# A conv's vector taps handed out two at a time, and its normalisation moved behind the compression step

## The chip, the cores and the metric

One core of a Trainium2 chip runs the whole program. The metric is the device time of one execution in microseconds (us), as the median of a few runs. The engines are TensorE (PE; its weight loads are PEld), VectorE (DVE), ScalarE (ACT), GpSimd (POOL), and SyncE (SP), whose queue issues the DMAs. Each engine works through its own queue in order and waits on semaphores for the others.

## The reference

One decoder layer over 1024 tokens of 1024 channels, float32. A normalised input `h` is projected once, and the columns feed three head groups:

```
proj = h @ w_in                                   # 1024 x 2712
p_conv, p_nsa, p_rwkv = split(proj)               # 512, 1304, 896 columns
# conv group: u, gate = split(p_conv)
y = causal_dwconv(u * sigmoid(gate), dw_w, dw_b)  # width 31, 256 channels
y = silu(layer_norm(y, ln_g, ln_b))               # over the 256 channels
# sparse attention (8 query heads, 2 KV heads): compressed, selected and windowed branches
# RWKV-7 (4 heads of 64): delta-rule state, group norm, gate
x = x + concat(y_conv, y_nsa, y_rwkv) @ w_out
x = x + (silu(dwconv3(h2 @ w_gate)) * (h2 @ w_up)) @ w_down
return rms_norm(x)
```

## The kernel before, in words

Channels lie on the 128 partitions, tokens along the free axis in two halves of 512. The kernel runs stage after stage: load and normalise `x`, project, attention tiles (with RWKV work between them), output projection, feed-forward. This change concerns the projections, from about 50 to 360 us.

A projection of 128 columns (`proj_T`, L235) is two PSUM banks, one for each half of the tokens, each of 24 matmuls on L229. Inputs and weights are held as a rounded part and a rest, so each of the eight slices of the inner dimension costs three matmuls. `wload` (L210) fetches the weights in two pieces of 256 KB; `split` (L118) makes the two parts of a piece: ACT copies to `whi` (L120), DVE subtracts to `wlo` (L121). There are two buffers of each, so a piece can be split only once the piece two before it has been used. Banks of projections rotate over two PSUM buffers, so a bank starts once the bank two before it has been copied out (for the keys by ACT on L689 and DVE on L690, for the queries by ACT on L818 and L120 and DVE on L121). I count the banks in order: 16 to 23 are the conv's, 24 to 27 the keys, 28 to 35 the queries, 36 and 37 the first piece of the second RWKV pair, 38 and 39 the first compression, 40 to 45 the other three.

The width-31 convolution covers two groups of 128 channels. Group 0 is 31 instructions on DVE over all 1024 tokens, one for each tap (L270, L272). Group 1 is shared: for each tap and each half ACT scales the input into one of two buffers `ctap` (L278), and POOL adds it to the sum (L279): 60 such pairs, after POOL's first tap (L274). So ACT's third scaling waits for POOL's first addition, and so on, and what stands behind it in ACT's queue waits too: weight copies and bank copies.

The normalisation over 256 channels follows for each half: PE sums both groups (L284), DVE subtracts the mean (L287), ACT squares (L289), PE sums (L294), DVE takes a reciprocal root and spreads it (L301), PE broadcasts (L303), then DVE and ACT finish (L306 to L310) and SP stores the result (`md`, L311).

RWKV work is traced with high priority in between: S00, S01 and so on prepare a pair of heads; each has a chain of 62 small POOL instructions (L532, L534) that inverts a triangular matrix, on data that comes back from DRAM (`sN`); V solves, C runs the state.

The order on each engine is not written by hand. A scheduler with its own cost model places the traced instructions, by the order of the string `steps`, priorities and dependences:

```
lora r0 S00 conv taps V00 S01 keys q C00 V01 r1a cmp0 r1b cmp1 r1c S10 C01 ...
```

Of the kernel before, what the change touches and what calls it, by code (L numbers as in the profile page):

```python
# [7 lines left out]
F32 = mybir.dt.float32  # L8
F32R = mybir.dt.float32r
I32 = mybir.dt.int32  # L10
AF = mybir.ActivationFunctionType
ALU = mybir.AluOpType
AX = mybir.AxisListType
PSUM = bass.MemoryType.PSUM
T = 1024
D = 1024
P = 128


class K:  # L20
    def __init__(self, tc, a, out, ctx, bufs=None):
        self.tc, self.nc, self.a, self.out, self.ctx = tc, tc.nc, a, out, ctx
        self.B = dict(b2=20, wraw=2, whi=2, wlo=2, t4=4, rraw=2, cy=2, hx=12, ev=3, cv=2, lora=2, rb=20, at=2, pr=7, rt=2,
                      QS=2, pp=6, q8=2, pT=5, xn=8, ds=((), (0, 1, 2), (3, 4), (5, 6, 7), (8, 9), (10,), (), ()), h2=14, graw=2, prod=5, ft=4, u=4, wr2=4, wfh=3, wfl=3, S=2, p1=2, om=6, grow=2, pre=2, ap=(), wf=("own", "wf", "om"), hd=("vector",) * 4, tq=((0, 1, 2, 3),), ttag=("tr", "rw"),
                      mm=3, tr=2, av=1, rw=2, mm1=2, tr1=2, pm=2, early="00 01", ga=2, gb=1, gc=1, y=16, r4=15, ta=3, tb=4, mid=2, de=dict(S3="gpsimd", T3="vector", T1="gpsimd", T2="gpsimd", T4="vector", S1="gpsimd", S2="gpsimd", S4="gpsimd"), order=(7, 6, 5, 4, 0, 3, 2, 1), sc=0, pk=1280, st="sync", last=5, sub="gpsimd",  steps="lora r0 S00 conv taps V00 S01 keys q C00 V01 r1a cmp0 r1b cmp1 r1c S10 C01 V10 S11 C10 V11 C11", both=0, cm="gpsimd", rpu=(), wo="vector", tap=(0, 31), vt="cv", vs="vector", va={1: (0, 1), 3: (2, 3), 5: (4, 5), 7: (6, 7)}, vq="sync", vl=1, vw=1, t1=("pm", "tr1"), into={6: (6, 2), 4: (4, 2), 3: (3, 1), 2: (2, 1), 1: (1, 1), 0: (0, 1)})
        self.B.update(bufs or {})
        P_ = lambda n, **k: ctx.enter_context(tc.tile_pool(name=n, **k))
        self.cst = P_("cst", bufs=1)
        self.sm = P_("sm", bufs=4)
        self.big = P_("big", bufs=1)  # L30
        self.mcp = tc.tile_pool(name="mc", bufs=1)
        self.mc = self.mcp.__enter__()
        self.dram = P_("dram", bufs=1, space=bass.MemoryType.DRAM)
        self.uid = 0
        self.st = getattr(tc.nc, self.B["st"])
        self.xp = self.psp = None
# [81 lines left out]
    def split(self, hi, lo, src, eng="vector"):  # L118

        self.nc.scalar.activation(hi, src, AF.Copy)  # L120
        getattr(self.nc, eng).tensor_tensor(lo, src, hi.bitcast(F32), op=ALU.subtract)  # L121

    def consts(self):
        nc = self.nc
# [85 lines left out]
    def wload(self, aps, n):  # L210

        nc = self.nc
        his, los = [], []
        for u in range(2):
            raw = self.wt([P, 4, n], "wraw")
            for i, ap in enumerate(aps):
                m = n // len(aps)
                nc.sync.dma_start(raw[:, :, i * m:i * m + m], ap[u * 512:u * 512 + 512].rearrange("(k p) m -> p k m", p=P))
            hi = self.wt([P, 4, n], "whi", F32R)
            lo = self.wt([P, 4, n], "wlo", F32R)  # L220
            self.split(hi, lo, raw)
            his += [hi[:, k, :] for k in range(4)]
            los += [lo[:, k, :] for k in range(4)]
        return his, los
# [19 lines left out]
    def conv_proj(self, hT):  # L244
        nc, w = self.nc, self.a["w_in"][0]
        self.cy = []
        for j in range(2):
# [10 lines left out]
            self.proj_T(w[:, j * P:(j + 1) * P], hT, cu)  # L258
            self.cy.append(y)

    def conv_rest(self):
        nc = self.nc
        acc = [self.t4(name="cacc")[:, 0:T] for _ in range(2)]
        for j in range(2):
            y, t = self.cy[j], acc[j]
            m = self.B["tap"][j]
            for d in range(31):
                w = self.cw[:, j, d:d + 1]
                if d >= m and d == 0:
                    nc.vector.tensor_scalar(t, y[:, 0:T], w, self.cb[:, j:j + 1], op0=ALU.mult, op1=ALU.add)  # L270
                elif d >= m:
                    nc.vector.scalar_tensor_tensor(t, y[:, d:d + T], w, t, op0=ALU.mult, op1=ALU.add)  # L272
                elif d == 0:
                    nc.gpsimd.tensor_scalar(t, y[:, 0:T], w, self.cb[:, j:j + 1], op0=ALU.mult, op1=ALU.add)  # L274
                else:
                    for o in (0, 512):
                        z = self.xt([P, 512], "cv", name="ctap")
                        nc.scalar.activation(z, y[:, o + d:o + d + 512], AF.Copy, scale=w)  # L278
                        nc.gpsimd.tensor_tensor(t[:, o:o + 512], t[:, o:o + 512], z, op=ALU.add)  # L279
        for half in range(2):  # L280
            sl = slice(half * 512, half * 512 + 512)
            pm = self.bank("tr1")
            for j in range(2):
                nc.tensor.matmul(pm, self.ones, acc[j][:, sl], start=j == 0, stop=j == 1)  # L284
            sq = []
            for j in range(2):
                nc.vector.scalar_tensor_tensor(acc[j][:, sl], pm, -1.0 / 256, acc[j][:, sl], op0=ALU.mult, op1=ALU.add)  # L287
                s = self.xt([P, 512], "cv", name="csq")
                nc.scalar.activation(s, acc[j][:, sl], AF.Square)  # L289
                sq.append(s)  # L290
            pv = self.bank("tr1")
            for i in range(4):
                for j in range(2):
                    nc.tensor.matmul(pv[:, i:i + 1], sq[j][:, i * P:(i + 1) * P], self.ones[:, 0:1], start=j == 0, stop=j == 1)  # L294
            v = self.small([P, 4], "cv")
            nc.vector.tensor_scalar(v, pv[:, 0:4], 1.0 / 256, 1e-5, op0=ALU.mult, op1=ALU.add)
            r = self.small([P, 4], "cr")
            self.rsqrt(r, v, [P, 4])
            dg = self.xt([P, 512], "cv", name="cdg")
            for i in range(4):  # L300
                nc.vector.tensor_scalar(dg[:, i * P:(i + 1) * P], self.idn, r[:, i:i + 1], None, op0=ALU.mult)  # L301
            pr = self.bank("tr1")
            nc.tensor.matmul(pr, self.ones, dg, start=True, stop=True)  # L303
# [521 lines left out]
    def attn_tile(self, i):  # L825
# [46 lines left out]
        for br, lo_k, M, vo in ((2, max(0, k1 - 640), self.mwin, 128), (1, 0, self.msel, 0)):  # L872
# [8 lines left out]
            for r in range(4):  # L881
# [7 lines left out]
                for c, (ka, kb) in enumerate(pcs):  # L889
# [6 lines left out]
                    for g in range(2):  # L896
                        pe.matmul(pts[g][:, 0:n], QS[:, r, g, :], KH[g][hf][:, ks], start=True, stop=False)  # L897
                        pe.matmul(pts[g][:, 0:n], QS[:, r, g, :], KL[g][hf][:, ks], start=False, stop=True)  # L898
                    o = ka % 512 - o
# [371 lines left out]

    def build(self):
        order = self.B["order"]
        nc, a = self.nc, self.a
        self.phase("1")
        self.consts()
# [5 lines left out]
        hT = self.T_tiles("hT", (self.x, "hx", self.B["hx"]))  # L1282
# [32 lines left out]
        def chain(j, h):  # L1315
            with self.tc.high_priority(offset=100000):
                self.rwkv_chain(us[j, h])
        steps = dict(lora=lambda: self.rwkv_lora(hT), keys=lambda: self.attn_keys(hT), q=lambda: self.attn_q(hT),
                     cmp=lambda: self.attn_cmp(hT), conv=lambda: self.conv_proj(hT), taps=self.conv_rest, r0=lambda: self.rwkv_proj(0, hT),
                     r1=lambda: self.rwkv_proj(1, hT), cmp0=lambda: self.attn_cmp(hT, (0,)), cmp1=lambda: self.attn_cmp(hT, (1,)),  # L1320
                     r1a=lambda: self.rwkv_proj(1, hT, (0,)), r1b=lambda: self.rwkv_proj(1, hT, (1,)), r1c=lambda: self.rwkv_proj(1, hT, (2,)))
        for st in self.B["steps"].split():
# [15 lines left out]
        grow = [self._t(self.x3, [P, 512], F32, "grow", None) for _ in range(2)]  # L1338
# [67 lines left out]
```

## Time and profile before

| | |
|---|---|
| median of 3 runs | 1483.7 us (1480.32 to 1494.8) |
| profiled execution | 1479.4 us |
| its span in the trace | 1477.5 us |
| PE busy | 1388.7 us (94%) |
| DVE, ACT, POOL busy | 1002.7, 686.9, 499.2 us |
| share of the last-ending chain: PE, DVE, POOL | 79%, 8%, 4% |

PE is busy nearly everywhere, so the span shortens only where PE waits or runs at the lower clock. Of the 40 slices of the page, the three from 148 to 258 us show a granted clock of 8 tenths, and the first of them PE at 5 tenths of busy time. They lie in the stage that the change edits.

### The profile page before, as it was taken

The page shows a single profiled execution, that of the slowest core. Times are in us where ns is not written, and L with a number is a line of the kernel's source. Part 1 is how long each engine was busy: PE and PEld are TensorE (multiplying, and loading weights), DVE is VectorE, ACT ScalarE, POOL GpSimd, SP SyncE. Part 2 cuts the span into 40 slices and gives each one's busy share as a digit, 9 for nine tenths or more (in the row PEclk, how much of TensorE's full clock was granted, in tenths as well). Part 3 has the DMA queues.
Part 4 walks back from the last instruction along what each step waited for, and adds up shares of the span by engine and source line. Part 5 has one row for each costly group of instructions (what it writes and reads, how often), then busy time and mean ns, then how long its engine had stood idle before and what let it go on. Part 6 is the DMA issues. An engine that isn't in the chain of part 4 may idle for free.

```text
span 1477.5 us, 22767 instructions
## 1 busy us (share of the span) xinstructions
PE 1388.7 (94%) x7897; PEld 1095.2 (74%) x7897; DVE 1002.7 (68%) x2187; ACT 686.9 (46%) x1377; POOL 499.2 (34%) x607
## 2 busy tenths in 40 slices
PE   6999589998899999999799899999999999999997
PEld 5887457776677676766588677888788788888886
DVE  6347594454868778798257867676775776666685
ACT  5441245624456665678223533343343333445463
POOL 1002996921144066220000144443444442113310
PEclk9999888999899999999899999999999999999999
DMA  6133133436514254542722123332332334986533
GB/s 185 40 107 82 44 103 111 142 84 179 153 33 139 78 154 125 181 150 81 240 89 83 43 93 93 108 107 70 104 113 93 108 100 162 388 280 216 188 92 114
DMA packets 206679, 186.69 MB, mean 126 GB/s; under 512 B 56355, under 2 KB 145764, under 8 KB 206564
## 3 DMA queue, kind: packets, MB, share of 16 engines
q1 hardware_dynamic: 206564, 185.24, 40.3%
q8 instruction: 62, 1.02, 0.3%
q14 instruction: 53, 0.43, 0.1%
HBM read 126.99 MB, written 58.20 MB: 125 GB/s over the span
## 4 chain that ended last, share of the span: by engine, by line
PE 79%; DVE 8%; POOL 4%; DMA 3%; ACT 2%; issue 2%; SPq 1%; ACTq 0%; DVEq 0%; POOLq 0%
PE gb L229 13%; PE mm L229 12%; PE rw L229 10%; PE ga L229 9%; PE gc L229 8%; PE tr L229 5%; PE tr L922 5%; PE av L930 4%; PE mm L897 2%; PE mm L898 2%; POOL sT L534 1%; POOL sx L532 1%; DVE pp L901 1%; POOL cacc L279 1%; DVE pp L915 1%
## 5 line engine op out<-in xcount | busy, mean ns | idle before, releaser
L229 PE MATMUL mm<-hT,whi 128*128 128x512 f32 x608 | 200.3, 409 | 19.6 <-DVE ev L690 14.8
L229 PEld LDWEIGHTS mm<-hT,whi 128*128 128x128 f32 x608 | 115.7, 193 | 48.9 <-ACT whi L120 20.2
L229 PE MATMUL mm<-hT,wlo 128*128 128x512 f32 x304 | 123.0, 407 | 1.9 <-DVE wlo L121 1.9
L925 ACT ACTIVATE pT<-tr 128x512 f32<-128x512 f32 (+1 forms) x152 | 79.9, 536 | 60.6 <-PE tr L922 59.2
L930 PE MATMUL av<-pT,V 128*64 128x128 f32 x1056 | 96.0, 287 | 1.5 <-ACT pT L925 1.5
L1076 POOL TENSOR_TENSOR S<-wraw,wr 128x512 f32<-128x512 f32 x22 | 28.5, 1296 | 192.8 <-DVE or L107 91.1
L922 PE MATMUL tr<-idn,pp 128*128 128x128 f32 x528 | 90.3, 289 | 1.8 <-DVE pp L915 1.8
L279 POOL TENSOR_TENSOR cacc<-cacc,ctap 128x512 f32<-128x512 f32 x60 | 85.1, 1429 | 12.7 <-ACT ctap L278 12.4
L121 DVE TENSOR_TENSOR sp<-rb,sp 128x512 fp32r<-128x512 f32 x66 | 55.6, 842 | 49.4 <-ACT sp L120 49.4
L229 PE MATMUL rw<-woh,mix 128*128 128x512 f32 x240 | 79.5, 407 | 9.0 <-ACT mix L120 9.0
L229 PE MATMUL rw<-sp,sp 128*128 128x512 f32 x330 | 86.0, 389 | 0.0
L229 PE MATMUL tr<-sp,sp 128*128 128x512 f32 x330 | 85.9, 389 | 0.0
L897 PE MATMUL mm<-KH,QS 128*128 128x512 f32 (+2 forms) x192 | 77.7, 411 | 3.1 <-DVE mx L901 2.8
L930 PEld LDWEIGHTS av<-pT,V 128*64 128x64 f32 x1056 | 59.2, 136 | 28.3 <-issue 13.7
L922 PEld LDWEIGHTS tr<-idn,pp 128*128 128x128 f32 x528 | 55.9, 141 | 30.5 <-issue 29.1
L915 DVE TENSOR_SCALAR pp<-pp,sm 128x640 f32<-128x640 f32 (+7 forms) x128 | 76.5, 638 | 0.9
L120 ACT ACTIVATE sp<-rb 128x512 fp32r<-128x512 f32 x66 | 41.6, 630 | 74.1 <-PE tr L229 36.5
L121 DVE TENSOR_TENSOR sp<-b,sp 128x512 fp32r<-128x512 f32 x88 | 72.1, 827 | 5.2 <-ACT sp L120 5.0
L229 PEld LDWEIGHTS mm<-hT,wlo 128*128 128x128 f32 x304 | 58.5, 193 | 18.1 <-DVE wlo L121 3.8
L229 PEld LDWEIGHTS tr<-sp,sp 128*128 128x128 f32 x330 | 61.9, 188 | 12.9
L229 PEld LDWEIGHTS rw<-sp,sp 128*128 128x128 f32 x330 | 61.9, 188 | 12.9
L532 POOL TENSOR_TENSOR sx<-sN,sT 128x60 f32<-128x60 f32 (+24 forms) x124 | 48.0, 387 | 63.0 <-DMA sN<-dn 54.9
(455 smaller groups left out, 3648.8 us busy)
## 6 DMA issues: line engine op xcount, KB each, us to landing
wr<-in_ffn_w_gate_dram SPq DMA_DIRECT2D x44, 256.0 KB
wraw<-in_ffn_w_up_dram SPq DMA_DIRECT2D x44, 256.0 KB
pdS<-prod SPq DMA_DIRECT2D x44, 256.0 KB
b<-pdS SPq DMA_DIRECT2D x44, 256.0 KB
rb<-tdT SPq DMA_DIRECT2D x44, 256.0 KB
pdA<-prod SPq DMA_DIRECT2D x33, 256.0 KB
b<-pdA SPq DMA_DIRECT2D x33, 256.0 KB
wraw<-in_w_in_dram SPq DMA_DIRECT2D x30, 256.0 KB
```

The costliest lines, as they stand in the source:

```text
L120: self.nc.scalar.activation(hi, src, AF.Copy)
L121: getattr(self.nc, eng).tensor_tensor(lo, src, hi.bitcast(F32), op=ALU.subtract)
L229: mm = lambda l, r, **k: self.nc.tensor.matmul(out, l, r, skip_group_check=more, **k)
L279: nc.gpsimd.tensor_tensor(t[:, o:o + 512], t[:, o:o + 512], z, op=ALU.add)
L532: v_.tensor_tensor(x, N[:, q, q + 1:32].unsqueeze(2).to_broadcast([P, n, w]), Tm[:, q, 0:w].unsqueeze(1).to_broadcast([P, n, w]), op=ALU.mult)
L897: pe.matmul(pts[g][:, 0:n], QS[:, r, g, :], KH[g][hf][:, ks], start=True, stop=False)
L898: pe.matmul(pts[g][:, 0:n], QS[:, r, g, :], KL[g][hf][:, ks], start=False, stop=True)
L915: v.tensor_scalar(Ps[g], Ps[g], sm[:, g:g + 1], None, op0=ALU.mult)
L922: pe.transpose(pt[:, o:o + P], Ps[g][:, kt * P:kt * P + P], self.idn)
L925: s.activation(pT[:, 0:n], pt[:, 0:n], AF.Copy)
L930: pe.matmul(av[g * 64:g * 64 + 64, r * P:r * P + P], self.V[kk // 2][:, kk % 2, vo + g * 64:vo + g * 64 + 64], pT[:, o:o + P], start=first ...
L1076: gp.tensor_tensor(t, x, y, op=op)
```

## The change

The conv taps become a step of their own. It takes the two accumulators, puts the 31 DVE taps of group 0 on a list and traces group 1 (ACT and POOL) at once, as before. Each later call of `wload` takes two taps off the list behind each of its two splits, with an edge that keeps them behind that split's DVE instruction. What is left of the list, and the normalisation, comes in a new step `cend` after `cmp0`: six banks, 40 to 45, are traced behind it.

```diff
-  steps="lora r0 S00 conv taps V00 S01 keys q C00 V01 r1a cmp0 r1b cmp1 r1c ..."
+  pace=2, steps="lora r0 S00 conv taps V00 S01 keys q C00 V01 r1a cmp0 cend r1b cmp1 r1c ..."
@@ split
-        getattr(self.nc, eng).tensor_tensor(lo, src, hi.bitcast(F32), op=ALU.subtract)
+        return getattr(self.nc, eng).tensor_tensor(lo, src, hi.bitcast(F32), op=ALU.subtract).ins
@@ wload
-            self.split(hi, lo, raw)
+            ins = self.split(hi, lo, raw)
+            if self.fill:
+                with self.tc.issue_after(ins):
+                    for f in self.fill[:self.B["pace"]]:
+                        f()
+                    del self.fill[:self.B["pace"]]
+    def conv_taps(self):
+        nc = self.nc
+        self.cacc = [self.t4(name="cacc")[:, 0:T] for _ in range(2)]
+        def dve(d):
+            y, t, w = self.cy[0], self.cacc[0], self.cw[:, 0, d:d + 1]
+            if d == 0:
+                nc.vector.tensor_scalar(t, y[:, 0:T], w, self.cb[:, 0:1], op0=ALU.mult, op1=ALU.add)
+            else:
+                nc.vector.scalar_tensor_tensor(t, y[:, d:d + T], w, t, op0=ALU.mult, op1=ALU.add)
+        self.fill = [lambda d=d: dve(d) for d in range(31)]
+        # group 1: the ACT and POOL loop of before, unchanged
     def conv_rest(self):
-        # both groups' taps
+        for f in self.fill:
+            f()
+        self.fill = []
+        acc = self.cacc
         # normalisation, unchanged
```

Lines behind the new code have higher numbers in the changed kernel (L272 becomes L277, L502 becomes L518, L711 becomes L727, L830 becomes L846, L947 becomes L963, L311 becomes L327).

What moves, first on DVE, from the conv's second projection on (`GA`, `GR`, `BK` belong to S00, `lw`, `cum`, `rn` to S01, `wlo` are splits, `cacc` the taps). Before:

```order
L121 TENSOR_TENSOR wlo_1460<-wraw_1457,whi_1459 128x512
L270 TENSOR_SCALAR cacc_1581<-cy_1383,par 128x1024
L272 SCALAR_TENSOR_TENSOR cacc_1581<-cy_1383,par,cacc_1581 128x1024
L502 TENSOR_TENSOR GA_1175<-pm_1193,gmask 128x256
L502 TENSOR_TENSOR GR_1177<-pm_1193,gmask 128x256
L272 SCALAR_TENSOR_TENSOR cacc_1581<-cy_1383,par,cacc_1581 128x1024
L502 TENSOR_TENSOR GA_1176<-pm_1194,gmask 128x256
L502 TENSOR_TENSOR GR_1178<-pm_1194,gmask 128x256
L516 TENSOR_TENSOR BK_1163<-BK_1163,rPC_1110 128x512
L272 SCALAR_TENSOR_TENSOR cacc_1581<-cy_1383,par,cacc_1581 128x1024 x3
```

and in the changed kernel at the same place:

```order
L121 TENSOR_TENSOR wlo_1460<-wraw_1457,whi_1459 128x512
L518 TENSOR_TENSOR GA_1175<-pm_1193,gmask 128x256
L518 TENSOR_TENSOR GR_1177<-pm_1193,gmask 128x256
L518 TENSOR_TENSOR GA_1176<-pm_1194,gmask 128x256
L518 TENSOR_TENSOR GR_1178<-pm_1194,gmask 128x256
L532 TENSOR_TENSOR BK_1163<-BK_1163,rPC_1110 128x512
L121 TENSOR_TENSOR wlo_1520<-wraw_1517,whi_1519 128x512
L121 TENSOR_TENSOR wlo_1526<-wraw_1523,whi_1525 128x512
L438 TENSOR_SCALAR lw_1876<-lw_1876 128x512
L440 SCALAR_TENSOR_TENSOR cum_1883<-rst,lw_1876 128x512
```

The taps have left this place: ahead of the copy of bank 24 (L690) stood 21 taps, now 4.

Then DVE between the query splits, in the changed kernel (`ev` are the rests of the query banks, `VA`, `rH` belong to the RWKV chain); before, no tap stood here:

```order
L121 TENSOR_TENSOR wlo_2430<-wraw_2426,whi_2429 128x512
L277 SCALAR_TENSOR_TENSOR cacc_1581<-cy_1383,par,cacc_1581 128x1024
L121 TENSOR_TENSOR wlo_2439<-wraw_2435,whi_2438 128x512
L277 SCALAR_TENSOR_TENSOR cacc_1581<-cy_1383,par,cacc_1581 128x1024 x2
L121 TENSOR_TENSOR ev_2420<-q_2417,ev_2419 128x512
L277 SCALAR_TENSOR_TENSOR cacc_1581<-cy_1383,par,cacc_1581 128x1024
L622 COPY rH_738<-rw_2599 64x64 x2
L121 TENSOR_TENSOR wlo_2516<-wraw_2512,whi_2515 128x512
```

This pattern goes on to the second compression split, where the last tap stands. POOL's order and the order of ACT's scalings among the bank copies stay nearly as they were: POOL's additions are interleaved with the S00 and S01 chains as before, and ahead of ACT's copy of bank 24 stand six scalings where five stood.

Last, the DMA queue at the start of attention (`V` ends the load of keys and values, `q` and `QS` feed the first tile, `ffn_w_down` pieces are for later, `md` is the conv's result). Before:

```order
L711 DMA V_4513<-vd 128x2x256
L830 DMA q_816_4515<-qd 128x4x128
L835 DMA QS_4517<-qd 64x4x128
L836 DMA QS_4517<-qd 64x4x128
L835 DMA QS_4517<-qd 64x4x128
```

and now:

```order
L727 DMA V_4513<-vd 128x2x256
L963 DMA whi_5595<-in_ffn_w_down_dram 128x512
L327 DMA md<-cth_568_3121 128x512
L963 DMA wlo_5597<-in_ffn_w_down_dram 128x512
L963 DMA wraw_5599<-in_ffn_w_down_dram 128x512
L963 DMA whi_5613<-in_ffn_w_down_dram 128x512
L963 DMA wlo_5615<-in_ffn_w_down_dram 128x512
L327 DMA md<-cth_570_3128 128x512
L846 DMA q_816_4515<-qd 128x4x128
L851 DMA QS_4517<-qd 64x4x128
```

The first tile's loads now stand behind five weight pieces and the last two stores of the conv.

## Rows read from the trace of the kernel before

**Rows 1.** Busy time by stage: stretch, length, then each engine busy (instructions), clock, DMA.

```profile
128.00:164.00 36.00, 36.00 (x175) 28.46 (x175) 34.86 (x44) 10.04 (x17) 22.96 (x25) 1.00 0.33 78
164.00:173.50 9.50, 2.08 (x9) 1.34 (x8) 0.00 (x0) 0.00 (x0) 7.62 (x26) 0.88 0.00 0
173.50:230.00 56.50, 38.09 (x179) 27.62 (x179) 47.59 (x48) 27.19 (x45) 49.82 (x42) 0.71 0.33 88
230.00:292.00 62.00, 62.00 (x374) 48.38 (x374) 24.76 (x35) 39.55 (x67) 54.51 (x60) 0.98 0.42 129
292.00:361.00 69.00, 68.41 (x439) 53.09 (x438) 35.84 (x107) 25.54 (x56) 13.20 (x42) 1.00 0.44 120
361.00:400.00 39.00, 30.16 (x189) 22.36 (x188) 29.45 (x102) 18.08 (x38) 7.00 (x13) 0.78 0.74 200
```

**Rows 2.** PE in time around its longest wait: start, length, what, [idle before, releaser].

```profile
165.69 0.39 PE L229 MATMUL mm<-hT,wlo 128*128 128x512 f32 x1
180.89 1.19 PE L229 MATMUL mm<-hT,whi 128*128 128x512 f32 x2 [14.81 <-DVE ev L690]
```

**Rows 3.** ACT in time, same columns: around that wait, and the last scaling.

```profile
176.16 0.72 ACT L278 ACTIVATE ctap<-cy,par 128x512 f32<-128x512 f32 x1 [19.16 <-POOL cacc L279]
179.44 0.58 ACT L689 ACTIVATE ev<-mm 128x512 fp32r<-128x512 f32 x1
...
288.17 0.72 ACT L278 ACTIVATE ctap<-cy,par 128x512 f32<-128x512 f32 x1
```

**Rows 4.** POOL in time: the S00 chain and the conv's first tap behind it.

```profile
139.16 0.72 POOL L532 TENSOR_TENSOR sx<-sN,sT 128x31 f32<-128x31 f32 x1 [42.47 <-DMA sN<-dn]
...
163.96 0.31 POOL L532 TENSOR_TENSOR sx<-sN,sT 128x76 f32<-128x76 f32 x1
...
173.47 1.20 POOL L274 TENSOR_SCALAR cacc<-cy,par 128x1024 f32<-128x1024 f32 x1
```

**Rows 5.** DVE in time: taps beside the S00 chain, and beside additions.

```profile
141.74 6.56 DVE L272 SCALAR_TENSOR_TENSOR cacc<-cy,par,cacc 128x1024 f32<-128x1024 f32 x5
...
188.70 2.39 DVE L272 SCALAR_TENSOR_TENSOR cacc<-cy,par,cacc 128x1024 f32<-128x1024 f32 x1
```

**Rows 6.** POOL in time, beside the second of those taps.

```profile
188.71 1.29 POOL L279 TENSOR_TENSOR cacc<-cacc,ctap 128x512 f32<-128x512 f32 x1
189.96 1.21 POOL L532 TENSOR_TENSOR sx<-sN,sT 128x24 f32<-128x24 f32 x1
191.13 1.28 POOL L279 TENSOR_TENSOR cacc<-cacc,ctap 128x512 f32<-128x512 f32 x1
```

**Rows 7.** The tile `cacc` by instruction: count, ns min/median/max, first and last start.

```profile
L279 POOL TENSOR_TENSOR cacc<-cacc,ctap x60: 1260/1292/2307, 174.9 to 290.0; 128x512 f32<-128x512 f32 x60
L272 DVE SCALAR_TENSOR_TENSOR cacc<-cy,par,cacc x30: 1269/1285/2386, 128.9 to 209.3; 128x1024 f32<-128x1024 f32 x30
```

**Rows 8.** Groups from 173.47 to 291.7 us: busy, mean ns, idle before, releaser.

```profile
L279 POOL TENSOR_TENSOR cacc<-cacc,ctap 128x512 f32<-128x512 f32 x60 | 85.1, 1429 | 12.7 <-ACT ctap L278 12.4
```

**Rows 9.** PE in time: the first and the twelfth matmul of bank 38.

```profile
292.58 1.02 PE L229 MATMUL mm<-hT,whi 128*128 128x512 f32 x2
...
295.52 0.39 PE L229 MATMUL mm<-hT,wlo 128*128 128x512 f32 x1
```

**Rows 10.** PE in time, from the last bank to the first tile.

```profile
360.48 0.40 PE L229 MATMUL mm<-hT,wlo 128*128 128x512 f32 x1
...
364.45 1.12 PE L415 MATMUL rw<-lora,lw_w 32*128 32x512 f32 x2
...
376.73 2.05 PE L843 MATMUL mm<-kcmp,q 128*128 128x128 f32 x8 [0.82 <-DMA q<-qd]
```

**Rows 11.** The DMA queue (SP) in time, at the first tile.

```profile
371.59 1.05 SPq L711 DMA_DIRECT2D V<-vd  x2
372.69 0.57 SPq L830 DMA_DIRECT2D q<-qd  x1
...
380.27 0.59 SPq L947 DMA_DIRECT2D whi<-in_ffn_w_down_dram  x1
```

More of the change, by code (lines that the diff above doesn't have):

```diff
@@ L23, in __init__ @@
         self.B = dict(b2=20, wraw=2, whi=2, wlo=2, t4=4, rraw=2, cy=2, hx=12, ev=3, cv=2, lora=2, rb=20, at=2, pr=7, rt=2,
-                      QS=2, pp=6, q8=2, pT=5, xn=8, ds=((), (0, 1, 2), (3, 4), (5, 6, 7), (8, 9), (10,), (), ()), h2=14, graw=2, prod=5, ft=4, u=4, wr2=4, wfh=3, wfl=3, S=2, p1=2, om=6, grow=2, pre=2, ap=(), wf=("own", "wf", "om"), hd=("vector",) * 4, tq=((0, 1, 2, 3),), ttag=("tr", "rw"),
-                      mm=3, tr=2, av=1, rw=2, mm1=2, tr1=2, pm=2, early="00 01", ga=2, gb=1, gc=1, y=16, r4=15, ta=3, tb=4, mid=2, de=dict(S3="gpsimd", T3="vector", T1="gpsimd", T2="gpsimd", T4="vector", S1="gpsimd", S2="gpsimd", S4="gpsimd"), order=(7, 6, 5, 4, 0, 3, 2, 1), sc=0, pk=1280, st="sync", last=5, sub="gpsimd",  steps="lora r0 S00 conv taps V00 S01 keys q C00 V01 r1a cmp0 r1b cmp1 r1c S10 C01 V10 S11 C10 V11 C11", both=0, cm="gpsimd", rpu=(), wo="vector", tap=(0, 31), vt="cv", vs="vector", va={1: (0, 1), 3: (2, 3), 5: (4, 5), 7: (6, 7)}, vq="sync", vl=1, vw=1, t1=("pm", "tr1"), into={6: (6, 2), 4: (4, 2), 3: (3, 1), 2: (2, 1), 1: (1, 1), 0: (0, 1)})
+                      QS=2, pp=6, q8=2, pT=5, pace=2, xn=8, ds=((), (0, 1, 2), (3, 4), (5, 6, 7), (8, 9), (10,), (), ()), h2=14, graw=2, prod=5, ft=4, u=4, wr2=4, wfh=3, wfl=3, S=2, p1=2, om=6, grow=2, pre=2, ap=(), wf=("own", "wf", "om"), hd=("vector",) * 4, tq=((0, 1, 2, 3),), ttag=("tr", "rw"),
+                      mm=3, tr=2, av=1, rw=2, mm1=2, tr1=2, pm=2, early="00 01", ga=2, gb=1, gc=1, y=16, r4=15, ta=3, tb=4, mid=2, de=dict(S3="gpsimd", T3="vector", T1="gpsimd", T2="gpsimd", T4="vector", S1="gpsimd", S2="gpsimd", S4="gpsimd"), order=(7, 6, 5, 4, 0, 3, 2, 1), sc=0, pk=1280, st="sync", last=5, sub="gpsimd",  steps="lora r0 S00 conv taps V00 S01 keys q C00 V01 r1a cmp0 cend r1b cmp1 r1c S10 C01 V10 S11 C10 V11 C11", both=0, cm="gpsimd", rpu=(), wo="vector", tap=(0, 31), vt="cv", vs="vector", va={1: (0, 1), 3: (2, 3), 5: (4, 5), 7: (6, 7)}, vq="sync", vl=1, vw=1, t1=("pm", "tr1"), into={6: (6, 2), 4: (4, 2), 3: (3, 1), 2: (2, 1), 1: (1, 1), 0: (0, 1)})
         self.B.update(bufs or {})
@@ L259, in conv_proj @@
             self.cy.append(y)
+    def conv_taps(self):
[8 more added lines that the diff above has]
+        self.fill = [lambda d=d: dve(d) for d in range(31)]
+        y, t = self.cy[1], self.cacc[1]
+        for d in range(31):
+            w = self.cw[:, 1, d:d + 1]
+            if d == 0:
+                nc.gpsimd.tensor_scalar(t, y[:, 0:T], w, self.cb[:, 1:2], op0=ALU.mult, op1=ALU.add)
+            else:
+                for o in (0, 512):
+                    z = self.xt([P, 512], "cv", name="ctap")
+                    nc.scalar.activation(z, y[:, o + d:o + d + 512], AF.Copy, scale=w)
+                    nc.gpsimd.tensor_tensor(t[:, o:o + 512], t[:, o:o + 512], z, op=ALU.add)
     def conv_rest(self):
         nc = self.nc
[L263 to L279, printed above, removed]
+        for f in self.fill:
+            f()
+        self.fill = []
+        acc = self.cacc
         for half in range(2):
@@ L1273, in build @@
         order = self.B["order"]
+        self.fill = []
         nc, a = self.nc, self.a
@@ L1318, in build @@
         steps = dict(lora=lambda: self.rwkv_lora(hT), keys=lambda: self.attn_keys(hT), q=lambda: self.attn_q(hT),
-                     cmp=lambda: self.attn_cmp(hT), conv=lambda: self.conv_proj(hT), taps=self.conv_rest, r0=lambda: self.rwkv_proj(0, hT),
+                     cmp=lambda: self.attn_cmp(hT), conv=lambda: self.conv_proj(hT), taps=self.conv_taps, cend=self.conv_rest, r0=lambda: self.rwkv_proj(0, hT),
                      r1=lambda: self.rwkv_proj(1, hT), cmp0=lambda: self.attn_cmp(hT, (0,)), cmp1=lambda: self.attn_cmp(hT, (1,)),
```

## The prediction

> **What bounds the kernel now.** I read the table of engines first: PE is busy for 94% of the span, so time can only come from where PE waits or runs at the lower clock. The busy time by stage then shows where that is around the change [rows 1]: from 128 to 164 us PE is full; from 164 to 230 us it is busy for 40 of 66 us, at a granted clock down to 0.71, which is a mix of the two levels; from 230 to 361 us it is full again; from 361 to 400 us it has 9 us of gaps.
>
> PE in time gives the largest hole: nothing from 166 to 181 us, released by DVE's part of the copy of bank 24 [rows 2]. That copy was late because ACT's part stood behind a scaling that had waited 19.16 us for POOL's addition [rows 3]. POOL was late because the first tap of its group stands behind 49 of the 62 instructions of the S00 chain, from 139.16 to 173.47 us [rows 4]. The first 24 of those took 24.8 us, the other 25 only 9.5 us, although the tiles are no smaller. What differs is DVE: beside the first 24 it ran taps back to back, beside the others it was idle [rows 1, 5].
>
> So taps and POOL hold each other up, and the rows show how. A tap beside the small chain instructions takes 1.31 us [rows 5], its undisturbed time (median 1.285, [rows 7]), and the chain instruction waits for its end. A tap beside an addition takes 2.39 us [rows 5]: 1.29 us of addition [rows 6], then itself, while POOL's next chain instruction shows 1.21 us [rows 6]. One addition and one tap together take 2.42 us (188.71 to 191.13, [rows 6]), which is the sum of both. They run one after the other.
>
> **Term 1: taps leave the S00 chain.** Ahead of the copy of bank 24 DVE had 21 taps and now has 4. At the pace of the undisturbed half (0.38 us each), 49 chain instructions take 19 us instead of 34.3. DVE keeps splits and S01 work there, and the four taps run near its end: I add 2.5 us for these (0 is one bound; the other is 9, four taps by 1.285 and five or six short instructions by about 0.7). So these 49 end at about 161 us instead of 173.5, **12.8 us earlier**, bounds 6.3 to 15.3. One more scaling stands ahead of ACT's copy now, one addition of 1.3 us. PE's hole of 14.81 us shrinks by about 11, to 4.
>
> **Term 2: the taps meet the additions instead.** Before, 10 taps ran from 174.9 us, where the additions start, to their end at 291; now 27 do. That is 17 more taps by 1.285 = 21.8 us, and as taps and additions alternate, it is 21.8 us more for the pair. In this stretch POOL was nearly always occupied: 60 additions took 85.1 us with waits inside them, and POOL idled 12.7 us ahead of them, waiting for ACT [rows 8]. Extra taps can use that idle time. So the end of the additions moves by 21.8 - 12.8 = +9.0 us if none of the 12.7 is used and by -3.7 us if all is. I take +4, as DVE was busy in part of those gaps.
>
> What hangs on it: ACT's order ties the weight copies to the scalings. Before, the last scaling (288.17 us, [rows 3]) stood ahead of the first weight copy of bank 38, and PE came to that bank 4.4 us later, at 292.58 [rows 9]: PE was the limit, by a few us. Now the last scaling stands ahead of the second weight copy, which bank 38 needs for its 13th matmul; that began before at about 295.8 [rows 9]. With 0.72 us for the scaling and about 1.4 us for the two halves of the split, it can begin at 288.17 + 2.1 + 4 = 294.3 us: **-1.5 us** for the projections so far, bounds -9.2 (shift -3.7) and +3.5 (shift +9.0). Most of what term 1 gives PE at 170 us, PE gives back by waiting for weights through the queries.
>
> Here a rule of the Trainium skill matters. By the rows, chain instructions cost DVE nothing, as taps beside them keep 1.31 us [rows 5]. The Trainium skill, "SBUF — State Buffer", Who interferes with whom, says that a DVE instruction with two SBUF inputs and a GpSimd instruction that reads SBUF exclude each other for the whole instruction, whichever starts first. Its sum would add the 14 + 24 chain instructions that lie between the additions, at the pace of the undisturbed half, 15 us; the first rows of DVE speak against that for short instructions, and agree with it for additions.
>
> **Term 3: the tail.** From bank 38 to the end of bank 45 PE was full [rows 1], with the normalisation beside it; its instructions there are the same now, so that stretch moves with term 2. PE's own pieces of the second half's normalisation, and the steps of V01, move behind the last bank, which shows their waits for ACT and DVE: 0 to 3 us. DMA: the first tile's `q` was issued 1.1 us behind the last `V`, landed and released PE at 376.73 us, 16 us behind the last bank [rows 10, 11]. Now five weight pieces and two stores stand between. An issue takes about 0.5 us [rows 11], so seven are 3.5 us, and the last store waits for DVE to finish the conv's normalisation. Against it, the hidden side: five pieces that came behind `q` (from 380.27 us, [rows 11]) are done by then, and bank 45 itself ends earlier by the PE pieces moved behind it (some 3 us, which the loads of keys also gain). I take **+2 us**, bounds -1 and +8 (all of 3.5, and 5 us of transfer ahead of `q`).
>
> Edits that cost nothing: the edges that hold the taps are on DVE alone, with no wait on another engine; taps are needed only by the normalisation, which now comes 22 us after the last tap. Group 1's loop is the same. RWKV's preparation S01 moves forward on DVE; POOL's part of it still stands between the same additions.
>
> **Sum.** -1.5 + 2 = +0.5 us on the profiled execution's 1479.4. It lies 4.3 us below the median of the runs (1483.7), so a new median would be between 1480 and 1484: I say **1482 us**, no change.
>
> **Rivals.**
>
> *PE keeps the time it regains (faster).* The additions could end well before 290, if ACT feeds POOL evenly and taps fall into POOL's gaps. PE would then be limited by its own work: it resumes at 170 instead of 181. From 173.5 to 230 us it lost 18.4 us of busy time [rows 1], 7.4 of it before 180.89, and ran at 0.71. Without any later wait it would be 11 + 11 = 22 us ahead. For it: PE was full from 230 us on, so POOL had some slack. Against it: there are 12.7 us of idle time for 21.8 us of taps [rows 8]. Half to all of 22 us, less 2 at the tail: 1460 to 1471. It decides if the additions end before 283 us. Chance 0.28.
>
> *POOL becomes the bound outright (slower).* Nothing of the idle 12.7 us is used, and the chain instructions hold up the taps too: 38 of them lie between the additions, by 0.38 us 15 us. The additions end at 291 + 9 = 300 to 315, and PE begins the 13th matmul of bank 38 at 299 to 314 instead of 295.8. With the middle of the chain's price that is +11, and +5 at the tail: 1495 to 1500 us, 1506 with all. It decides if they end after 303 us. For it: DVE and POOL are both near full from 173.5 to 230 us [rows 1], and DVE's slack after 230 is where 20 taps now go. Against it: taps of 1.31 us beside the chain [rows 5]. (This is the lock that the Trainium skill's page on SBUF states.) Chance 0.20.
>
> *The taps don't move.* The order of instructions shows them between the splits; chance 0.01.
>
> **How the numbers follow.** My forecast is the first case, chance 0.51, from 1472 to 1492 (terms 2 and 3 at their bounds, on 1480 to 1484). About 1% (14.8 us: faster is below 1468.9, slower above 1498.5) is what a measurement tells from no change. Faster takes three quarters of the first rival and a little of the forecast, 0.22; slower half of the second rival and some of the forecast's tail, 0.14; the rest, 0.64, is no change. The range leaves out some of either rival's far end: 1461 to 1500.
>
> **What would show it.** Right on term 1: the S00 chain's first 24 instructions take 9 to 15 us instead of 24.8, and PE's hole at 166 us is 3 to 6 us. Right on term 2: taps between query splits take 2.3 us, POOL's additions start near 162 us and end between 288 and 300 us, and PE, full before from 230 us, shows waits for `whi` and `wlo` on L229 between 175 and 290. Right on term 3: PE's first tile (L843 before) still waits for `q`, 16 to 22 us after the last bank. Wrong: additions that end before 283 us, or PE waits in the queries that sum to less than 5 us; or a last bank that ends after 368 us.

## The result

The changed kernel takes 1500.3 us (median of 16 runs, 1495.1 to 1513.0), the kernel before 1482.3 us in the same comparison (1480.3 to 1494.8). The ratio is 1.0111, with a 95% interval of 1.0092 to 1.0130: slower by 1.1%, some 16 us. The prediction was no change, 1482. The profiled execution of the changed kernel takes 1497.4 us with a span of 1495.7, 18.0 us more than the one before.

Stages of the changed kernel; the first two are stretches of [rows 1], the last two are new (stretch, length, PE, PEld, DVE, ACT and POOL busy, clock, DMA):

```profile
128.00:164.00 36.00, 36.00 (x177) 28.82 (x176) 15.87 (x35) 9.95 (x17) 21.61 (x50) 1.00 0.34 78
173.50:230.00 56.50, 48.77 (x313) 38.28 (x312) 52.73 (x51) 30.79 (x53) 55.12 (x38) 0.86 0.40 107
345.00:372.00 27.00, 20.76 (x185) 16.18 (x181) 12.06 (x34) 10.72 (x22) 5.34 (x11) 0.66 0.81 242
450.00:745.00 295.00, 268.63 (x2290) 193.42 (x2290) 225.51 (x738) 177.19 (x419) 89.73 (x123) 0.94 0.45 141
```

The last two stretches in the kernel before:

```profile
345.00:372.00 27.00, 23.08 (x206) 18.06 (x204) 6.71 (x16) 12.57 (x28) 4.48 (x11) 0.88 0.72 219
450.00:745.00 295.00, 277.69 (x2354) 202.54 (x2352) 222.46 (x750) 180.90 (x431) 90.88 (x123) 0.97 0.47 146
```

Around the taps the change does what it says: DVE is busy for 15.87 us beside the S00 chain (34.86 before, [rows 1]), and PE has 10.7 us more work done from 173.5 to 230. The loss shows where the diff changes nothing: from 450 to 745 us PE is busy for 9 us less and at a lower clock.

POOL in time (chain start, its 25th instruction, the conv's first tap):

```profile
138.71 0.48 POOL L548 TENSOR_TENSOR sx<-sN,sT 128x31 f32<-128x31 f32 x1 [41.94 <-DMA sN<-dn]
148.02 0.31 POOL L548 TENSOR_TENSOR sx<-sN,sT 128x76 f32<-128x76 f32 x1
...
162.51 1.36 POOL L283 TENSOR_SCALAR cacc<-cy,par 128x1024 f32<-128x1024 f32 x1
```

The first 24 chain instructions take 9.3 us (24.8 before) and the first tap starts 11 us earlier than in [rows 4].

PE's two largest waits from 164 to 345 us (in total, times, longest), and the tile `cacc`:

```profile
PE mm L235 <- DVE ev L706: 6.9, 2, 5.2
PE mm L235 <- DVE wlo L121: 5.9, 5, 2.8
```

```profile
L288 POOL TENSOR_TENSOR cacc<-cacc,ctap x60: 1257/1461/2282, 164.1 to 286.5; 128x512 f32<-128x512 f32 x60
L277 DVE SCALAR_TENSOR_TENSOR cacc<-cy,par,cacc x30: 1271/1644/2315, 156.4 to 290.3; 128x1024 f32<-128x1024 f32 x30
```

The hole of 14.81 us [rows 2] is 5.2 us now. A tap's median has grown from 1.285 to 1.644 us and an addition's from 1.292 to 1.461 [rows 7], yet the last addition starts 3.5 us earlier.

PE at the last projection matmul, at the end of V01's solution and at the first attention tile, in the changed kernel:

```profile
347.74 0.77 PE L235 MATMUL mm<-hT,wlo 128*128 128x512 f32 x1
...
360.97 1.14 PE L595 MATMUL rw<-W,sN 64*64 64x64 f32 x16 [0.68 <-ACT W L592]
...
372.10 2.06 PE L859 MATMUL mm<-kcmp,q 128*128 128x128 f32 x8
```

and V01's end in the kernel before:

```profile
363.38 1.14 PE L579 MATMUL rw<-W,sN 64*64 64x64 f32 x16 [0.68 <-ACT W L576]
```

So the projections end 12.7 us earlier than in [rows 10], V01's solution 2.4 us earlier, the first tile starts 4.6 us earlier. Up to here the changed kernel is ahead.

But the lead does not reach S10, the preparation that comes behind V01. ACT in the changed kernel, then in the kernel before:

```profile
364.47 0.63 ACT L325 ACTIVATE cth<-cz 128x512 f32<-128x512 f32 x1 [2.27 <-DMA md<-cth]
365.12 0.65 ACT L597 ACTIVATE VA<-rw 64x256 f32<-64x256 f32 x2
365.80 0.69 ACT L433 ACTIVATE lw<-rw,par 128x512 f32<-128x512 f32 x1
```

```profile
365.61 0.69 ACT L417 ACTIVATE lw<-rw,par 128x512 f32<-128x512 f32 x1 [0.40 <-PE rw L415]
```

ACT's first step of S10 (`lw`) now stands behind a step of the moved normalisation that waits for the conv's store, and starts 0.2 us later than before.

From here RWKV's units run in series: S10 (the third preparation) stores its matrices `dn`; C01, C10 and C11 (the state chains) each end by storing a gated head-half `gz`, and the output projection reads all of them. The DMA queue, before and after:

```profile
391.95 1.82 SPq L507 DMA_DIRECT2D dn<-GA  x4
462.35 0.33 SPq L642 DMA_DIRECT2D md<-gz  x1
600.42 0.36 SPq L642 DMA_DIRECT2D md<-gz  x1
697.10 0.34 SPq L642 DMA_DIRECT2D md<-gz  x1
```

```profile
402.44 2.01 SPq L523 DMA_DIRECT2D dn<-GA  x4
482.12 0.32 SPq L658 DMA_DIRECT2D md<-gz  x1
631.46 0.33 SPq L658 DMA_DIRECT2D md<-gz  x1
717.32 0.34 SPq L658 DMA_DIRECT2D md<-gz  x1
```

and the first long run of the output projection in the chain of waits (start, length, engine, line), before and after:

```profile
725.87 23.75 PE rw L229 x93
```

```profile
743.93 23.91 PE rw L235 x93
```

S10 is 10.5 us late, the last gated head-half 20.2, the output projection 18.1, which is as much as the whole difference between the two executions. The last `gz` marks how late the phase is; it is not shown to be what ends last. DVE in the changed kernel, directly ahead of it:

```profile
715.14 0.69 DVE L121 TENSOR_TENSOR wol<-wraw,woh 128x512 fp32r<-128x512 f32 x1 [4.05 <-ACT woh L120]
715.81 0.69 DVE L654 TENSOR_TENSOR gz<-gz,bv 128x512 f32<-128x512 f32 x1
```

The last `gz` stands behind a split of the output projection's weights that waits 4.05 us. The chain of waits runs through such weight pieces and the DMA queue from 707 to 725 us; in the kernel before it runs through the last tile's store at 704.50 us.

DVE shows how S10 came to be late. First the kernel before, then the changed one:

```profile
374.31 0.43 DVE L443 COPY cum<-rrn 128x512 f32<-128x512 f32 x1
...
379.01 0.42 DVE L452 TENSOR_SCALAR tha<-tha 128x512 f32<-128x512 f32 x1
379.35 0.68 DVE L848 TENSOR_TENSOR cmp<-mm,mcmp 128x512 f32<-128x512 f32 x1
```

```profile
374.26 0.69 DVE L864 TENSOR_TENSOR cmp<-mm,mcmp 128x512 f32<-128x512 f32 x1 [0.20 <-PE mm L859]
374.87 0.16 DVE L114 TENSOR_TENSOR rs_t<-rrn 128x8 f32<-128x8 f32 x1
...
375.15 0.68 DVE L867 TENSOR_REDUCE cmx<-cmp 128x8 f32<-128x512 f32 x1
...
376.15 0.90 DVE L116 SCALAR_TENSOR_TENSOR rrn<-rs_t,rrn 128x8 f32<-128x8 f32 x1
...
377.58 0.42 DVE L459 COPY cum<-rrn 128x512 f32<-128x512 f32 x1
```

The copy of the reciprocal root to `cum`, behind S10's short Newton steps (they refine that root), started at 374.31 us; now it starts at 377.58, because the first tile's additions and reductions stand between these steps. They stand there in the order fixed ahead of the run: before, the tile's first row on DVE came behind S10's `tha`; now it is in the middle of the Newton steps. I take it that the projections' earlier end lets the scheduler expect the tile earlier against S10, which waits for V01; the scheduler's own times are not on record, so this is not shown.

### The profile page after: what moved, and what is told of

Read it like the earlier page. It is cut to its first block, busy times and chain, and to the rows that moved or that the text cites. A ratio compares the mean times of both kernels' runs of the same rounds, so it can differ in the third digit from the quotient of the medians.

```text
span 1495.7 us, 22758 instructions
## 1 busy us (share of the span) xinstructions
PE 1404.2 (94%) x7897; PEld 1107.5 (74%) x7897; DVE 1018.4 (68%) x2187; ACT 688.3 (46%) x1377; POOL 504.7 (34%) x607
## 4 chain that ended last, share of the span: by engine, by line
PE 73%; DVE 13%; POOL 5%; DMA 4%; issue 3%; ACT 2%; SPq 1%; DVEq 0%; ACTq 0%
PE gb L235 12%; PE rw L235 10%; PE mm L235 10%; PE ga L235 9%; PE gc L235 8%; PE tr L235 5%; PE tr L938 4%; PE av L946 4%; POOL cacc L288 2%; DVE pp L917 2%; DVE pp L931 2%; PE mm L913 2%; PE mm L914 1%; POOL sT L550 1%; POOL sx L548 1%
## 5 line engine op out<-in xcount | busy, mean ns | idle before, releaser
L288 POOL TENSOR_TENSOR cacc<-cacc,ctap 128x512 f32<-128x512 f32 x60 | 96.4, 1620 | 2.1 <-ACT ctap L287 2.0
L121 DVE TENSOR_TENSOR wlo<-wraw,whi 128x512 fp32r<-128x512 f32 x55 | 48.2, 878 | 41.2 <-ACT whi L120 39.0
L235 PEld LDWEIGHTS mm<-hT,wlo 128*128 128x128 f32 x304 | 59.0, 194 | 22.7 <-DVE wlo L121 8.4
L931 DVE TENSOR_SCALAR pp<-pp,sm 128x640 f32<-128x640 f32 (+7 forms) x128 | 73.2, 612 | 0.9
```

The costliest lines, as they stand in the source:

```text
L121: return getattr(self.nc, eng).tensor_tensor(lo, src, hi.bitcast(F32), op=ALU.subtract).ins
L235: mm = lambda l, r, **k: self.nc.tensor.matmul(out, l, r, skip_group_check=more, **k)
L931: v.tensor_scalar(Ps[g], Ps[g], sm[:, g:g + 1], None, op0=ALU.mult)
```

## The experiments

To compare orders I count the attention tiles' DVE rows that stand ahead of the stores of the second, third and fourth `gz` (equal rows that follow one another count as one). The columns `dn` and `gz` are from one profiled execution each. The us are medians, all ratios are against the kernel before run beside them.

| kernel | rows ahead | `dn` of S10 | last `gz` | us | ratio, 95% |
|---|---|---|---|---|---|
| before | 115, 304, 462 | 392 | 697 | 1482.3 | |
| changed | 135, 343, 462 | 402 | 717 | 1500.3 | 1.0111 [1.0092, 1.0130] |
| e1 | 94, 291, 439 | 389 | 696 | 1483.3 | 1.0001 [0.9979, 1.0023] |
| e2 | 137, 345, 464 | 400 | 724 | 1500.6 | 1.0121 [1.0073, 1.0169] |
| e3 | 135, 341, 461 | 405 | 723 | 1493.0 | 1.0063 [1.0040, 1.0086] |
| e4 | 131, 336, 467 | 401 | 721 | 1502.2 | 1.0126 [1.0082, 1.0170] |
| e5 | 65, 250, 411 | 389 | 702 | 1496.5 | 1.0064 [1.0034, 1.0095] |
| e6 (on before) | 94, 291, 439 | 392 | 694 | 1479.6 | 0.9977 [0.9952, 1.0003] |
| e7 | 111, 303, 461 | 393 | 701 | 1483.3 | 1.0000 [0.9982, 1.0018] |
| e8 (on before) | 164, 371, 462 | 425 | 713 | 1493.6 | 1.0057 [1.0028, 1.0087] |
| e9 | 64, 229, 390 | 373 | 673 | 1487.8 | 1.0026 [1.0004, 1.0047] |
| e10 (on before) | 64, 250, 411 | 379 | 676 | 1475.3 | 0.9948 [0.9930, 0.9966] |
| e11 | 92, 291, 439 | 398 | 707 | 1487.5 | 1.0021 [1.0002, 1.0041] |
| e12 | 63, 242, 393 | 378 | 679 | 1489.2 | 1.0034 [1.0006, 1.0061] |

The count alone does not give the time: e5 and e10 have all but the same counts and lie 21 us apart.

**e1: the first tile behind S10's whole preparation.** `u.hold` is set in `rwkv_mats` at the masked products `G`, so it names the last one; `issue_after` orders instructions of one engine only.

```
+ u.hold = v.tensor_tensor(G[hp]..., op=ALU.mult).ins
- self.attn_tile(i)
+ if n == 0:
+     with self.tc.issue_after(us[1, 0].hold):
+         self.attn_tile(i)
+ else:
+     self.attn_tile(i)
```

> The changed kernel, with one edge more: on VectorE the first attention tile's instructions come behind the last masked product (GR) of the third head-half's preparation (S10). Theory O (order): the 18 us are lost because the change lets the scheduler put 43 VectorE rows of the first tile ahead of the end of S10's preparation (19 before the change), so that its matrices are stored at 402.4 us instead of 391.9, and because 12 weight subtractions for the down projection then fall inside the fourth preparation's elimination on GpSimd. With the edge none of the tile's rows is ahead and the subtractions stand outside the long part of the elimination. Theory O expects S10's matrices stored by 390, the last gated head-half stored by 700 (717 in the changed kernel), the output projection's first long run of matmuls by 729 (744), and a time of 1476 to 1486. Rival T (the tiles): the attention phase is bound by its own softmax on VectorE, and the first tile's start, 4.7 us earlier than before, is only a lead that the lower clock eats; then a tile held back starts 8 to 15 us later and the time is 1500 or more, up to 1512.

```profile
389.20 1.82 SPq L523 DMA_DIRECT2D dn<-GA  x4
```

1483.3 us. One edge that touches neither taps nor normalisation takes back 17 of the 18 us, so the loss lies in the order from the first tile on; rival T falls.

**e2: the same edge at the middle of the preparation** (`u.hold` at `tha`).

> The changed kernel, with the first tile's VectorE instructions behind the middle of S10's preparation only (its last row on tha), where they stood before the change: 11 to 20 of the tile's rows are ahead of the masked products, as in the kernel before (10 to 19), but the 12 subtractions on GpSimd stay inside the fourth elimination. Theory O: S10's matrices are stored near 392 as before, so the first 10 us of the delay are gone; the fourth elimination still takes some 42 us instead of 26, so that part of the loss stays: 1484 to 1494. If only the first cause counts it is 1480 to 1484; rival T expects 1498 to 1506.

A miss: 1500.6 us, no gain. S10's Newton steps run undisturbed again, but its products still come late:

```profile
400.48 1.80 SPq L523 DMA_DIRECT2D dn<-GA  x4
...
723.58 0.51 SPq L658 DMA_DIRECT2D md<-gz  x1
```

20 rows of the tile stand ahead of them, 19 before the change, so S10's own rows do not set its time: it starts 3.6 us later than in the kernel before (`rn` at 375.46 us, 371.82 before) and stores 8.5 us later. In the later units the order stays that of the changed kernel (137, 345, 464), and the last `gz` is 26.5 us late.

**e3: GpSimd's subtractions out of the fourth elimination.** `u.el` is the elimination's last step (its line is left out here).

```
- with self.tc.issue_after(self.cm_ins):
+ with self.tc.issue_after(us[1, 1].el if n == 3 else self.cm_ins):
```

> The changed kernel, with the 12 weight subtractions of the fourth tile (GpSimd) held behind the last step of the fourth elimination (S11), nothing else: the first tile's rows still stand inside S10's preparation. Theory O: S10's matrices stay at 402 us and S11's at 553, but the elimination behind them takes 24 to 28 us instead of 42, so that the solution is stored near 590 instead of 605; the time falls by what was lost there, to 1486 to 1496. If the elimination has slack (the stores before were 40 us apart, the last head-half only 20) it stays at 1497 to 1502. Rival T expects 1498 to 1503.

1493.0 us, 7 below the changed kernel. The subtractions are a part of the loss, not all. The elimination takes 25.5 us there (POOL, 569.9 to 595.4), 43.1 in the changed kernel and 27.4 in the kernel before. The profiled execution took 1502.5 us, 9.5 us above the median, so its rows don't show by which way the 7 us come back.

**e4: four taps behind each split** (`pace=4`).

> The changed kernel with four taps in place of two behind each split of weights, the normalisation where the change puts it. In the resulting order 3 to 14 of the first tile's rows stand ahead of S10's masked products, though 12 subtractions still lie inside the fourth elimination. Theory O: S10's matrices are stored by 394 and the time is 1482 to 1494, much like the run that holds the tile behind tha. A rival P (pace) says that the taps themselves cost what is lost, more of them behind a split hold back more splits: the projections end later than the 348.5 us of the changed kernel and the time is 1500 to 1510.

1502.2 us. The expectation of theory O (1482 to 1494) missed, and P gets the figure for another reason than it gave: the projections end 5 us before those of the kernel before (355.43 us, 360.48), not late against them, and the rows ahead (131, 336, 467) are near those of e2. After e2 and e4 I gave up S10's own rows as the measure and counted the rows ahead of each later unit (theory C).

**e5: the normalisation behind r1c** (`cend` moved three places on in `steps`).

> The changed kernel with the normalisation's step moved from behind cmp0 to behind r1c, the last projection; the taps as changed. Theory C (chain): through the attention phase the end is set by one serial chain, the RWKV head-halves (preparation, solution, state chain one after the other, in two PSUM banks), and each of its VectorE steps stands in the queue behind those attention rows that the scheduler put ahead of it. Counted in the order, the attention rows ahead of the stores of the second, third and fourth gated head-half are 115, 304, 462 in the kernel before, 135, 343, 462 in the changed one, 94, 291, 439 where the tile was held behind the whole preparation (1483), and 65, 250, 411 here. Theory C expects the last gated store by 690 (697 before, 717 changed) and a time of 1470 to 1484. Rival N (normalisation): what the change loses is the normalisation beside the last banks; put even later, its store of the conv rows comes later and the time is 1498 to 1510.

A miss for theory C: 1496.5 us with few rows ahead. The queue of SP shows what differs:

```profile
396.47 0.50 SPq L327 DMA_DIRECT2D md<-cth  x1
397.01 0.57 SPq L846 DMA_DIRECT2D q<-qd  x1
```

The first tile's query load stands in the queue behind the normalisation's last store, and the tile starts at 405 us. The stage table of the same run (columns as above):

```profile
372.00:406.00 34.00, 27.24 (x123) 20.47 (x124) 21.23 (x65) 5.60 (x11) 7.41 (x23) 0.50 0.48 109
```

PE runs there at a granted clock of 0.50, the lower level throughout. So a tile that starts too late seems to cost as well, as the filler beside the chain; no run changes this start alone.

**e6: the edge of e1 on the kernel before.**

> The kernel before with the same edge that cured the changed one: the first tile's VectorE rows behind the last masked product of S10's preparation. The attention rows ahead of the gated stores are then 94, 291, 439, the same as in that run, so the pair differs by the taps and the normalisation alone. Theory C with the prediction's first two terms right: the changed kernel under this edge is 1 to 5 us faster than this one, which gives 1483 to 1488. If the rows ahead decide alone, 1478 to 1484. Rival: the edge is worth in itself some 15 us, whatever the taps do: 1465 to 1470.

1479.6 us, not told apart from before. So the edge shows no gain by itself, and what it gives back in e1 is what the change lost. With the same rows ahead (94, 291, 439) the changed kernel e1 is 3.7 us slower, within the two intervals. The change shows no gain of its own.

**e7: the edge at the first four masked products**, on the changed kernel, which makes the rows ahead nearly those of the kernel before.

> The changed kernel, with the first tile's VectorE rows behind the first four of the eight masked products of S10's preparation. The attention rows ahead of the gated stores are 111, 303, 461 here, nearly the kernel before's 115, 304, 462, where the run that held the tile behind tha had 137, 345, 464 and 1500.6. Theory C expects the time of the kernel before, 1480 to 1487, with the last gated store at 695 to 702. Rival D (downstream): what cured the first run was the subtractions of GpSimd or the late first tile; then a hold that is 12 rows shorter gives something between, 1488 to 1500.

1483.3 us, ratio 1.0000. e2 and e7 differ in where one edge stands, by 26 and 42 rows ahead of the second and third `gz`, and by 17 us. Of the twelve subtractions 3 stand inside the elimination in e7, 6 in e1, 12 in e2, so e7 undoes most of both parts. Against e3, where the elimination is as short (25.5 us, 28.9 in e7), e7 is 10 us faster: that much is left for the rows.

**e8: twenty DVE rows more in S10 (8.7 us by themselves), on the kernel before.**

```
  tt(kk, kk, pb, op=ALU.mult)
+ if (j, h) == (1, 0):
+     for _ in range(20):
+         v.tensor_scalar(kk, kk, 1.0, None, op0=ALU.mult)
```

> The kernel before with 20 multiplications of the normalised key by 1.0 (128x512, some 0.43 us each on VectorE, 8.7 us together) put into S10's preparation, which is about what the change delays it by (391.9 to 402.4 us). Attention rows ahead of the gated stores: 164, 371, 462. Theory C: the delay of one link is not absorbed by the attention tiles beside it; the last gated store moves to 712 to 730 and the time to 1495 to 1515. Rival T (the tiles): the attention phase is bound by VectorE's and TensorE's total work; 8.7 us on an engine that is 68% busy move the time by 0 to 6 us, to 1482 to 1489.

A ratio of 1.0057, 8.5 us (4 to 13); the time (1493.6) lies between the ranges of theory C and rival T. The edit did more than it was meant to: the scheduler set the twenty rows among the tile's, from 378.25 to 406.77 us, and S10's matrices are stored at 424.60 us, 32.7 later than before, the last `gz` 16.0 later. So half of S10's delay is absorbed by then. Neither S10's delay nor the rows ahead measure the loss: the delay (32.7 us against 10.5) and the first two counts (164 and 371 against 135 and 343) are larger here than in the changed kernel, and the loss is smaller.

**e9 and e10: S10 in the two other PSUM banks**, on the changed kernel and on the kernel before (`early="00 01 10"`).

> The changed kernel, with S10's preparation in the two PSUM banks (pm) that the first two preparations use, in place of the two (rw) that V01's solution and C01's state chain use; nothing else. Theory C (the head-halves in series set the end): S10's preparation no longer stands between V01's solution and C01 in the same two banks, so its matrices are stored by 375 us (402.4 in the changed kernel) and C01's gated head-half by 455 (482). Attention rows ahead of the gated stores: 64, 229, 390 (changed 135, 343, 462). In the order the first tile's query load stands behind the store of S10's matrices on the DMA queue, so the first tile may start as late as 380. Theory C expects 1465 to 1482. Rival Q (queue): as in the run with the normalisation behind r1c, a late first tile leaves TensorE without filling work at the lower clock: first tile after 395 and 1485 to 1498.

> The kernel before, with S10's preparation in the two pm banks, as in the run beside it. Here the first tile's query loads stand ahead of the store of S10's matrices. Attention rows ahead of the gated stores: 64, 250, 411 (115, 304, 462 in the kernel before). Theory C: S10's matrices are stored by 380 (391.9), the last gated head-half by 685 (697), the time is 1462 to 1478. If the end of the attention phase is set by TensorE's own work once the chain is some microseconds shorter, 1476 to 1482.

e10 is the fastest of all, 1475.3 us. The last `gz` comes 21 us earlier, the time only 8: the chain of waits now runs through the last tile's own end (its store at 715.88 us). On the changed kernel the same edit gives 1487.8, 12 us more than e10. Both from 345 to 372 us, e9 first:

```profile
345.00:372.00 27.00, 27.00 (x215) 22.12 (x213) 13.52 (x42) 7.69 (x17) 1.98 (x6) 0.68 0.81 239
```

```profile
345.00:372.00 27.00, 24.53 (x245) 19.82 (x244) 14.50 (x37) 14.09 (x35) 5.65 (x11) 0.95 0.73 218
```

In e9 the last projection matmul runs at 349.3 us, and mostly small matmuls follow; in e10 projection matmuls stand between them until 363.6 us. Two stretches of e9 behind its last projection:

```profile
350.00:355.00 5.00, 5.00 (x81) 4.94 (x79) 2.85 (x10) 3.12 (x8) 1.81 (x6) 0.70 0.78 197
355.00:365.00 10.00, 10.00 (x60) 7.98 (x58) 3.09 (x14) 2.14 (x5) 0.00 (x0) 0.50 0.75 236
```

**e11: all taps behind the first split, with e1's edge** (`pace=31`).

> The changed kernel with all 31 taps let go behind the first split of weights (pace 31 in place of 2) and the first tile held behind S10's preparation as in the run that gave 1483; the attention rows ahead of the gated stores are 92, 291, 439, as there (94, 291, 439). So the pair differs by the pace alone. With four taps behind each split the projections ran 4 us ahead of the kernel before at their 900th matmul, with two 16 us. Theory C: a lead of the projections doesn't reach the end, because V01's solution waits for C00 and the elimination on GpSimd, which are 2 to 3 us ahead in either: 1480 to 1488. Rival P (pace): what the projections lose is lost at the end too: 1490 to 1500.

1487.5 us, in theory C's range; 4 us above e1, and the intervals overlap. The pace decides little. (`dn` and `gz` of e11 are from an execution 8 us above its median.)

**e12: e9 with the conv's stores issued by ScalarE.**

```
- self.st.dma_start(self.md[:, j, sl], th)
+ nc.scalar.dma_start(self.md[:, j, sl], th)
```

> The changed kernel with S10's preparation in the pm banks, and the four stores of the normalised conv rows issued by ScalarE in place of SyncE. In the run with the pm banks alone the first tile's query load stood right behind the last of these stores on SyncE's queue and behind the store of S10's matrices, was issued at 379.96 us, and TensorE began the tile at 383.6, the kernel before at 376.7; between 345 and 372 us its granted clock was 0.68 (0.88 before). Theory Q (queue): the late stores of the moved normalisation hold the query loads; without them the load is issued by 372, the tile starts by 376, and the time falls from 1487.8 to 1476 to 1483. Rival V (the chain's start): what is missing is V01's solution, which is no more than 2 to 3 us earlier than in the kernel before though the projections end 12 us earlier; then the queue changes nothing that lasts and the time stays at 1485 to 1490.

1489.2 us: the stores are not what holds the query load. It is issued even later, at 384.04 us (379.96 in e9), behind S10's `dn`. So whether a late load costs the time was not tried. That it is V01's start (rival V) agrees with the rows but was not tried by itself either.

## Why the prediction was wrong

Term 1 was right: 9.3 us for the first 24 chain instructions (9 to 15 said), the hole 5.2 us (3 to 6), the tap 11.0 us earlier (12.8, bounds 6.3 to 15.3).

Term 2 was mis-sized. The additions' end moved by -3.5 in place of +4, at the bound where all of POOL's idle time is used (2.1 us are left of 12.7, [rows 8]); a tap's median was 1.644 us, not 2.3. The waits for weights came (5.9 us for `wlo`), and PE gave back part of its lead: by ACT's copies it stood 16.5 us ahead at the fourth query bank (234.42 us) and 6.5 at bank 36 (280.55). But I let the last scaling set the 13th matmul of bank 38 and so took -1.5 for the projections, -9.2 at most; PE waits for weights (`wlo`) for 1.2 us in all from 275 to 300 us, and the projections end 12.7 us earlier. So the first rival, in which PE keeps the time it regains, came true in part as far as the projections' end, though neither of its marks held: the additions end behind 283 us, and the waits sum to more than 5 us.

Term 3 is the step that failed, and with it the sum. It priced the tail up to the first tile (+2, at most +8) and, without a reason, put nothing for what comes behind it: everything there was to move rigidly with the tile. In fact the tail is 8.1 us longer (16.3 us from last projection matmul to first tile in [rows 10], 24.4 now; PE runs at 0.66 from 345 to 372 us, 0.88 before), so the tile starts 4.6 us earlier, with no DMA wait shown; and behind it 22.7 us are lost. The terms as measured are -12.7 + 8.1 + 22.7 = 18.1 us, in place of -1.5 + 2 + 0. I had read the order only as far as the first tile. There the projections and the series part: the -12.7 us are -2.4 at V01's solution and nothing at S10's start, the tile's rows stand ahead of S10's in DVE's queue, and the second and third `gz` stand behind 20 and 39 more rows. e1 and e7 show by taking it away that the loss lies in this order, and e6 that the edge of e1 shows no gain by itself. e2 shows that putting S10's own rows back does not suffice, e3 that GpSimd's subtractions are some 7 us of it; some 10 are left for the rows (e7 against e3). How these divide among the units, and why e8 loses less behind more rows, stays open.

The slower rival was not it either. "POOL becomes the bound" gave a similar time (1495 to 1500) by a mechanism that did not occur: the additions end well before 303 us.

The Trainium skill, "PSUM — Partial Sum Buffer", Engine vs sequencer instructions, says that VectorE's and GpSimdE's queues are strictly first in, first out. The trace agrees in this place: the Newton step at 374.87 us follows the tile's addition of 0.69 us at 374.26, which stands ahead of it in the order. The Trainium skill, "SBUF — State Buffer", Who interferes with whom, says that a DVE instruction with two SBUF inputs contends with a GpSimd instruction that reads SBUF. The trace agrees in direction: with more taps beside the additions both medians are longer, 1.461 us for additions (1.292 before) and 1.644 for taps (1.285).

## What to carry to other kernels

Where a scheduler fixes the order ahead of the run, follow the order to the end of every serial chain, not only past the changed lines: time gained by filling work can put that work ahead of the chain in a queue. Count the filler's rows ahead of each link before and after: a change in these counts is a place to look, not yet a time (e5 and e10). And when a stage gains time, ask whether the next stage's start gained it too: here 12.7 us became nothing at S10.

## What the runs showed of the hardware

A PE that the profile shows busy all the time need not have the full clock. In e9 it is busy for 27.00 of 27 us at 0.68, a mix of the two levels (1.2 and 2.4 GHz): 1.00 up to 350 us, while projection matmuls run, then 0.70, and 0.50, the lower level, from 355 to 365 us, with mostly small matmuls and no gap shown. In e10 it is busy for 24.53 us at 0.95, with projection matmuls between the small ones. I had taken a full PE for one at full speed.
